# The first block of a fused two-layer product: first strip of w1 in five pieces, x's fourth tile as fp16 on another queue, wide products before narrow ones

## The chip, the core and the metric

The kernel runs on one core of a Trainium2 chip. The metric is the device time of one execution in microseconds (us), as the median of several runs; lower is better. A core has TensorE (PE in the rows; PEld is its weight load), VectorE (DVE), ScalarE (ACT), GpSimd (POOL) and SyncE (SP). SP, ACT and POOL can issue transfers (DMAs), each on a queue of its own, and all queues are served by the same 16 DMA engines.

## The reference

```python
x: (16, 512, 768)   w1: (768, 3072)   b1: (3072,)   w2: (3072, 768)      # all float32
y = np.matmul(x, w1) + b1
y = np.maximum(y, 0)
return np.matmul(y, w2).astype(np.float32)
```

## The kernel before

x is one matrix of 8192 x 768. Its rows are taken in 8 blocks of 1024, and the hidden width of 3072 in two chunks of 1536, so there are 16 iterations. In each of them a first layer (from x and w1 to y, with the bias and the maximum) is followed by a second layer (from y and w2 to the output). From the second iteration on both layers use fast matrix multiplication: DVE builds sums of blocks of x, w1, y and w2, and PE multiplies the sums (lines L1101 for the first layer, L1229 for the second). These sums need all blocks of a matrix, which at the start are not there yet, so the first layer of the first block is computed plainly (`first_block`, matmuls at L998) while the data come in.

What the first block needs, and the names that the rows use:

- The 1024 rows of x are 8 tiles of 128 rows. Tiles 0 to 3 (`rows`, kept in `s`) are loaded as fp32, tiles 0 and 2 by SP's queue, 1 and 3 by ACT's (L722). PE transposes each tile in six 128x128 pieces (L938), three to a bank of PSUM; DVE turns the first bank into fp16 (`x<-ps`, L946), ACT the second (L944). Tiles 4 to 7 (`xn`) come by POOL's queue, which converts fp32 to fp16 on the way, two tiles in a transfer (L717).
- The first chunk of w1 is six strips of 768 x 256 (`v1`), which POOL's queue converts to fp16 as well (L696). A strip is six blocks of 128 rows (k2 = 0 or 1, three k each). Strips 0 and 1 come in two halves, the others whole.
- w2 comes as twelve pieces behind them (L702), then the next block of x (L717).
- A strip gives two column groups of y (j = 0, 1). For each, six weight blocks are multiplied with x's tiles 0 to 3 (m = 0) and later with tiles 4 to 7 (m = 1). `plain(strip, j, m, parts)` records that: with parts = 2 the four tiles are two matmuls of 256 columns for each weight block, with parts = 1 one matmul of 512 columns. ACT then adds the bias and takes the maximum (L1006). For strips 0 and 1 the steps for k2 = 0 are put ahead of those for k2 = 1 (`split`).
- While it waits for the first tile PE multiplies a tile of ones (L739).

The order of the work is not written out by hand alone. `first_block` and the others record tasks in PE's order; a planner (`Graph.run`) places all tasks in time by a cost of each, and times at which data of the start are expected are given to it as `presets`. Each engine then runs its tasks in the planned order and waits on semaphores, so that these times move no transfer; they only set which task stands ahead of which on DVE and ACT. The transfers of the start are issued in `prologue`, in the order in which they are written there. POOL's queue has eight semaphores, and its ninth transfer is issued when the first has landed.

`constants` makes the unit matrices for the transposes, the tile of ones and, with eight fills on POOL (L681, L682), two tables of limits that a check of the input's size uses at the end of the kernel.

Of the kernel before, what the change touches and what calls it, by code (L numbers as in the profile page):

```python
# [131 lines left out]
LAST_POOL = (0, 1, 3)  # L132

EARLY = 5

# [460 lines left out]
class Fast:  # L596
# [66 lines left out]
    def constants(self):  # L663
        nc = self.nc
        nw1, nw2, nx, nb = self.NCH * 12, self.NCH * 16, self.M // P, self.H // P
        self.ident = self.const.tile([P, P], FP32, name="ident")
# [9 lines left out]
        self.high = self.const.tile([P, n], FP32, name="high")  # L676
        self.low = self.const.tile([P, n], FP32, name="low")
        at = 0
        for width, hi, lo in ((nw1, W1_HI ** 4, W1_LO ** 4), (nw2, W2_HI ** 2, W2_LO ** 2),
# [32 lines left out]
    def load_x(self, it, half, parts=1):  # L712
        m0 = self.block(it) * self.MB + half * 512
        r = self.xf[m0:m0 + 512, :].rearrange("(s p) k -> p s k", p=P)
        for n in range(parts):
            a, b = 4 // parts * n, 4 // parts * (n + 1)
            self.nc.gpsimd.dma_start(out=self.xn[:, 4 * half + a:4 * half + b], in_=r[:, a:b])  # L717

    def prologue(self):
# [18 lines left out]
        for _ in range(9):  # L738
            nc.tensor.matmul(self.ps[:, 7, 0:P], lhsT=self.ones, rhs=self.ones, start=True,  # L739
                             stop=True)  # L740

    def presets(self):
        g = self.g
        for t, at in enumerate((9.45, 11.45, 13.45, 15.45, 17.45, 24.0)):
            for k in range(2):
                g.preset(("w1", t // 3, 2 * (t % 3) + k), at - (0 if t > 1 or k else 0.9))
        for q in range(4):
            for h in range(3):
                for n in range(2):
                    g.preset(("w2", 2 * q + n, h), 25.05 + 3 * q + h + (0.3 if 3 * q + h > 5 else 0))  # L750
        for s in range(4):
            g.preset(("xn", 4 + s), 19.35 if s < 2 else 21.95)
            g.preset(("xn", s), 39.5)
            g.preset(("rows", s), (5.3, 5.3, 7.2, 7.2)[s])
        g.preset("b1_rows", 6.0)
# [167 lines left out]
    def add_transpose_first(self, half, s):  # L923

        for a in range(2):
            ps = Reg("ps", leaves=0)

            def view(ps=ps):
                p = self.ps[:, ps.at[0], :]
                if half:  # L930
                    p = p[:, 0:3 * P // 2].bitcast(FP16)
                return p[:, 0:3 * P].rearrange("p (k m) -> p k m", k=3)

            def turn(a=a, view=view):
                ident = (self.ident, self.ident16)[half]
                rows = self.xn[:, 4 + s, :] if half else self.s[:, s]
# [11 lines left out]
            self.g.add("PE", 210 if half else 380, turn, writes=[ps],  # L948
                       reads=[("xn", 4 + s)] if half else [("rows", s), self.hold[s]])
# [3 lines left out]
    def add_bias(self):  # L953
# [7 lines left out]
        def tables(after):  # L961
# [22 lines left out]
        return tables  # L984

    def plain(self, strip, j, m, parts=1, split=False):
# [37 lines left out]
    def first_block(self):  # L1024
        for s in range(4):
            self.add_transpose_first(0, s)
            if s == 1:
                tables = self.add_bias()
# [24 lines left out]
        for p in late[1:]:  # L1053
            next(p)
        run(*late, self.plain(1, 1, 1, 2),
            *(self.plain(strip, j, 1, 2 if strip == 2 else 1)
              for strip in range(2, EARLY) for j in range(2)))
        run(*(self.plain(strip, j, m) for strip in range(EARLY, 6) for m in range(2)
              for j in range(2)))

# [483 lines left out]
    def build(self):  # L1544
        self.place_all()
        self.plan()
        self.g.run(begin=5.0)
        return self
# [60 lines left out]
```

## Time and profile before

| | us |
|---|---|
| median of 3 runs | 846.82 (846.67 to 847.12) |
| the profiled execution | 846.81 |
| its span, from the first to the last instruction | 845.1 |
| PE busy | 838.5 (99%) |
| DVE busy | 735.7 (87%) |
| ACT busy | 567.3 (67%) |
| the first matmul of the second layer starts at | 41.23 |

The profile is that of one execution. Its own time is 1.7 us above its span, and 0.01 us below the median, so that a sum made on the profile can be held against the median as it is. An engine that is 99% busy sets the time where nothing but its own work stands between its instructions; what it waits for has to be read in the stretch where it waits.

### The profile page before, as it was taken

Reading aid. Unit: us, or ns where it says so; the run is one execution under the profiler, and the core shown is the slowest. Engines: PE = TensorE matmul, PEld = TensorE weight load, DVE = VectorE, ACT = ScalarE, POOL = GpSimd, SP = SyncE. Lnnn points to the kernel's source line nnn. Section 1 sums busy time; section 2 is a strip of 40 time slices with the busy share of each in tenths; the row PEclk is TensorE's granted clock in tenths of the full one; section 3 lists DMA queues with packets and bytes.
Section 4 is the critical chain, followed back from the end, with each engine's and each line's share of the span. In section 5 each row is a group of like instructions: output and inputs, shape, how many; then the busy total and the mean of one; then the engine's idle time right before and its main releaser. Section 6 shows DMA issues by size and latency. Waiting matters only on the chain.

```text
span 845.1 us, 16822 instructions
## 1 busy us (share of the span) xinstructions
PE 838.5 (99%) x6383; PEld 625.4 (74%) x6383; DVE 735.7 (87%) x1229; ACT 567.3 (67%) x1199; POOL 172.5 (20%) x186
## 2 busy tenths in 40 slices
PE   9999999999999999999999999999999999999997
PEld 7668778686786867768687686877868678686874
DVE  5899988969789697988999979798896979979787
ACT  4866876779677684856858568766757666456462
POOL 6210011102011010110031503324041240501303
PEclk9999999999999999999999999999999999999999
DMA  9997498978988678593893977979789797986926
GB/s 210 205 180 189 84 221 115 166 180 132 215 113 162 158 133 190 104 226 136 238 176 67 190 127 123 186 106 178 127 128 147 118 172 113 143 138 76 177 86 169
DMA packets 171127, 128.93 MB, mean 153 GB/s; under 512 B 93964, under 2 KB 169508, under 8 KB 171044
## 3 DMA queue, kind: packets, MB, share of 16 engines
q0 software_dynamic: 56592, 68.82, 53.2%
q1 hardware_dynamic: 113984, 58.02, 29.0%
q8 instruction: 50, 0.82, 0.4%
q10 hardware_dynamic: 468, 1.00, 0.3%
q14 instruction: 33, 0.27, 0.1%
HBM read 73.54 MB, written 69.21 MB: 169 GB/s over the span
## 4 chain that ended last, share of the span: by engine, by line
PE 99%; DMA 1%; ACT 0%; issue 0%; ACTq 0%
PE ps L1229 48%; PE ps L1101 47%; PE ps L998 4%; DMA s<-in_x_dram 1%; PE ps L938 1%; ACT s L1240 0%; PE ps L958 0%; PE ps L1427 0%; PE ps L1438 0%; ACTq L1240 0%
## 5 line engine op out<-in xcount | busy, mean ns | idle before, releaser
L1229 PE MATMUL ps<-v,y 128*128 128x384 f16 x2496 | 408.2, 326 | 0.0
L1101 PE MATMUL ps<-x,v 128*128 128x256 f16 x3600 | 395.6, 273 | 0.0
L1101 PEld LDWEIGHTS <-v 128*128 128x128 f16 x3600 | 352.2, 98 | 42.3
L1229 PEld LDWEIGHTS <-y 128*128 128x128 f16 x2496 | 244.2, 98 | 159.9
L1240 ACT ACTIVATE s<-ps 128x384 f32<-128x384 f32 (+1 forms) x245 | 153.1, 643 | 125.4 <-PE ps L1229 124.9
L1073 DVE TENSOR_TENSOR y<-y 128x768 f16<-128x768 f16 (+1 forms) x384 | 219.0, 617 | 2.5
L1144 DVE CUSTOM_DVE_ANT_0 y<-ps,s 128x512 f16<-128x512 f32 x240 | 155.9, 685 | 52.9 <-ACT s L1141 40.1
L1281 POOL DMA_DIRECT2D out_dram<-s x78 | 93.9, 1475 | 144.8 <-ACT s L1240 91.8
L1141 ACT ACTIVATE s<-ps,bt 128x256 f32<-128x256 f32 x180 | 75.1, 469 | 62.8 <-PE ps L1101 56.5
L841 DVE TENSOR_TENSOR x<-x 128x768 f16<-128x768 f16 (+1 forms) x210 | 113.4, 577 | 1.2
L1141 ACT ACTIVATE y<-ps,bt 128x256 f16<-128x256 f32 x180 | 69.4, 485 | 10.8 <-PE ps L1101 10.8
L1240 ACT ACTIVATE ps<-ps 128x384 f32<-128x384 f32 (+1 forms) x143 | 67.0, 507 | 6.5 <-PE ps L1229 3.2
L1246 DVE TENSOR_TENSOR s<-ps,s 128x768 f32<-128x768 f32 x74 | 70.5, 952 | 0.9
L717 POOL DMA_DIRECT2D xn<-in_x_dram x30 | 25.9, 863 | 213.3 <-DMA x<-xn 101.0
L1246 DVE TENSOR_TENSOR s<-s,ps 128x768 f32<-128x768 f32 x60 | 57.0, 950 | 2.1
L780 ACT ACTIVATE junk<-xn 128x768 f16<-128x768 f16 x64 | 53.9, 843 | 0.3
L1284 POOL DMA_DIRECT2D out_dram<-s x15 | 17.8, 1184 | 168.6 <-ACT s L1240 156.9
L1141 ACT ACTIVATE ps<-ps,bt 128x256 f32<-128x256 f32 x60 | 26.7, 445 | 32.4 <-PE ps L1101 31.4
L1137 ACT ACTIVATE ps<-ps 128x512 f32<-128x512 f32 x60 | 35.3, 588 | 4.8 <-DVE y L1144 4.0
L1152 DVE TENSOR_TENSOR s<-s,ps 128x512 f32<-128x512 f32 x30 | 20.6, 687 | 17.8 <-PE ps L1101 17.8
L998 PE MATMUL ps<-x,v 128*128 128x256 f16 (+1 forms) x216 | 31.8, 308 | 0.0
L1147 DVE SCALAR_TENSOR_TENSOR s<-ps,bt,s 128x256 f32<-128x256 f32 x60 | 26.1, 476 | 4.4 <-PE ps L1101 4.4
(61 smaller groups left out, 310.0 us busy)
## 6 DMA issues: line engine op xcount, KB each, us to landing
out_dram<-s POOLq DMA_DIRECT2D x93, 384.0 KB, 8.6
out_dram<-s SPq DMA_DIRECT2D x69, 384.0 KB, 7.0
xn<-in_x_dram POOLq DMA_DIRECT2D x28, 768.0 KB, 9.6
v<-in_w_dram POOLq DMA_DIRECT2D x16, 192.0 KB, 7.6
x<-out_dram SPq DMA_DIRECT2D x14, 192.0 KB, 2.4
w1d<-in_w_dram POOLq DMA_DIRECT2D x6, 384.0 KB, 6.6
w2d<-in_w_dram POOLq DMA_DIRECT2D x12, 192.0 KB, 5.0
v<-w1d SPq DMA_DIRECT2D x12, 192.0 KB, 4.8
```

The source lines that it names most:

```text
L780: self.nc.scalar.activation(out=self.junk, in_=self.xn[:, s, :], func=ACTF.Square, accum_out=self.stat[:, self.stat_at["x"] + i:][:, 0:1])
L841: self.nc.vector.tensor_tensor(out=self.two(x, out), in0=self.two(x, in0), in1=self.two(x, in1), op=ALU.add if sign > 0 else ALU.subtract)
L998: nc.tensor.matmul(self.ps[:, ps.at[0], cols], lhsT=self.v1[:, gi, 2 * h + k2, k, j * P:(j + 1) * P], rhs=rhs, start=(first and k2 == 0 an ...
L1073: self.nc.vector.tensor_tensor(out=self.two(self.y, out), in0=self.two(self.y, in0), in1=self.two(self.y, in1), op=ALU.add if sign > 0 els ...
L1101: nc.tensor.matmul(self.ps[:, at, j * self.QM:(j + 1) * self.QM], lhsT=self.v1[:, gi, self.w1s[c][gi][FIRST_V[p]], k, j * P:(j + 1) * P], ...
L1137: nc.scalar.activation(out=out, in_=ps, scale=float(a), func=func if kind == "out" else ACTF.Copy)
L1141: nc.scalar.activation(out=out[:, j], in_=ps[:, j], func=func, scale=float(a), bias=beta(j))
L1144: nc.vector._custom_dve(TENSOR_ADD_SAT, out=out, in0=ps, in1=s, s0=F_MAX, s1=0.0)
L1229: nc.tensor.matmul(self.ps[:, bank[ch].at[j], 0:NH], lhsT=self.y[:, ys[SECOND_U[p]], m0:m0 + P], rhs=self.v2[:, slot[SECOND_V[p]], h, :], ...
L1240: nc.scalar.activation(out=out, in_=ps, func=ACTF.Copy, scale=float(a))
L1246: engine.tensor_tensor(out=out, in0=in0, in1=in1, op=ALU.add if a == b else ALU.subtract)
L1281: nc.gpsimd.dma_start(out=rows, in_=out, accum_op=ALU.add)
```

## The change

All of it lies in the first block.

- x's tile 0 is loaded in two halves of 384 columns, one by SP's queue and one by ACT's. Tiles 1 and 2 both go by SP's queue. Tile 3 goes by POOL's queue, behind the first piece of w1, and is converted to fp16 on the way; its transposes and copies are then fp16 like those of tiles 4 to 7.
- Strip 0 of w1 comes in five pieces: blocks 0, 1, 2 and 3 of 128 rows one by one, blocks 4 and 5 together. Strips 1 and 2 come in halves, the others whole. All six strips stand ahead of x's tiles 4 to 7 (before, the last strip stood behind them).
- The eight fills of the limit tables move behind all these issues (`limits`).
- The products of strip 0 are a function of their own, `plain_first`. The first block of weights is multiplied with tiles 0 to 2 as soon as it is there (256 and 128 columns), then tile 3 is transposed, and the parts of tile 3 follow by themselves (128 columns); the second half of the strip is done 512 columns at a time.
- Strips 1 and 2 are done 512 columns at a time for tiles 0 to 3. For tiles 4 to 7, nine of the twelve column groups take 256 columns at a time (before, six).
- The matmuls of ones are 4 of 256 columns, where they were 9 of 128.

```diff
     def prologue(self):
         nc = self.nc
-        for s in range(4):
-            (nc.sync, nc.scalar)[s % 2].dma_start(out=self.s[:, s],
-                                                  in_=self.xf[s * P:(s + 1) * P, :])
-            if s == 1:
-                self.load_bias()
+        for q, a in ((nc.sync, 0), (nc.scalar, self.K // 2)):
+            q.dma_start(out=self.s[:, 0, a:a + self.K // 2], in_=self.xf[0:P, a:a + self.K // 2])
+        for s in (1, 2):
+            nc.sync.dma_start(out=self.s[:, s], in_=self.xf[s * P:(s + 1) * P, :])
+        self.load_bias()
         self.constants()
-        self.load_strip(self.v1, 0, 0, 0, 2)
-        self.load_strip(self.v1, 0, 0, 1, 2)
-        for strip in range(2, EARLY):
-            self.load_strip(self.v1, 0, *divmod(strip, 3))
+        v = self.v1[:, 0, 0:2].rearrange("p a k h -> p (a k) h")
+        w1r = self.w1.rearrange("(k p) h -> p k h", p=P)
+        for k, n in ((0, 1), (1, 1), (2, 1), (3, 1), (4, 2)):
+            nc.gpsimd.dma_start(out=v[:, k:k + n], in_=w1r[:, k:k + n, 0:2 * P])
+            if k == 0:
+                nc.gpsimd.dma_start(out=self.row_tile(3), in_=self.xf[3 * P:4 * P, :])
+        for h in (1, 2):
+            self.load_strip(self.v1, 0, 0, h, 2)
+        for h in range(3):
+            self.load_strip(self.v1, 0, 1, h)
         self.load_x(0, 1, 2)
-        for strip in range(EARLY, 6):
-            self.load_strip(self.v1, 0, *divmod(strip, 3))
+        self.limits()
...
+    def plain_first(self):
...
+        for k in range(3):
+            for j in range(2):
+                product(j, 0, k, ((0, 2), (2, 1)))
+            if k == 0:
+                self.add_transpose_first(0, 3)
+        for j in range(2):
+            for k in range(3):
+                product(j, 0, k, ((3, 1),))
+        for j in range(2):
+            product(j, 1, 0, ((0, 4),))
+        for j in range(2):
+            for k in (1, 2):
+                product(j, 1, k, ((0, 4),))
...
-        for strip in range(2):
-            pair = [self.plain(strip, j, 0, 2, True) for j in range(2)]
-            for p in 4 * pair:
+        self.plain_first()
+        for strip in (1, 2):
+            pair = [self.plain(strip, j, 0, 1, True) for j in range(2)]
+            for p in 2 * pair:
                 next(p)
             run(*pair)
-        early = [self.plain(strip, j, 0, 2 if strip == 2 else 1)
-                 for strip in range(2, EARLY) for j in range(2)]
+        early = [self.plain(strip, j, 0) for strip in range(3, 6) for j in range(2)]
```

POOL, at the start of the program, before: the fills of the limit tables (`high`, `low`), then the issues of w1 (`v_65`), of x's tiles 4 to 7 (`xn`) and of the last strip.

```order
L669 CAST ident_88<-ident 128x128
L681 MEMSET high 128x24
...
L682 MEMSET low 128x24
L696 DMA v_65<-in_w_dram 128x3x256 x4
L696 DMA v_65<-in_w_dram 128x6x256 x3
L717 DMA xn<-in_x_dram 128x2x768 x2
L696 DMA v_65<-in_w_dram 128x6x256
L702 DMA v_66<-in_w_dram 128x2x384 x12
```

The same place after the change.

```order
L667 CAST ident_88<-ident 128x128
L736 DMA v_65<-in_w_dram 128x256
L738 DMA s<-in_x_dram 128x768
L736 DMA v_65<-in_w_dram 128x256 x3
L736 DMA v_65<-in_w_dram 128x2x256
L698 DMA v_65<-in_w_dram 128x3x256 x4
L698 DMA v_65<-in_w_dram 128x6x256 x3
L719 DMA xn<-in_x_dram 128x2x768 x2
L683 MEMSET high 128x24
```

The first issue of w1 now follows the unit matrices directly; one issue of x (`s`, tile 3) has come in behind it, and the last strip has moved ahead of `xn`.

PE, at the start of the program, before: the ones, the transposes of tiles 0 and 1, the bias, the transposes of tiles 2 and 3, then the first products.

```order
L739 MATMUL ps<-ones 128x128 x9
L938 MATMUL ps<-ident,s 128x128 x12
L958 MATMUL ps<-ident,b_rows 128x24
L938 MATMUL ps<-ident,s 128x128 x12
L998 LDWEIGHTS v_65
L998 MATMUL ps<-x,v_65 128x256
```

The same place after the change.

```order
L751 MATMUL ps<-ones 128x256 x4
L953 MATMUL ps<-ident,s 128x128 x12
L973 MATMUL ps<-ident,b_rows 128x24
L953 MATMUL ps<-ident,s 128x128 x6
L1008 LDWEIGHTS v_65
L1008 MATMUL ps<-x,v_65 128x256
L1008 LDWEIGHTS v_65
L1008 MATMUL ps<-x,v_65 128x128
...
L953 LDWEIGHTS s
L953 MATMUL ps<-ident_88,s 128x128
```

Six transposes of fp32 have gone from ahead of the first product; the fourth tile's transposes now stand behind the first block's products, as fp16, and PE waits there for that tile.

DVE, from the end of the bias tables on, before: sums of w1 (`v_65`), copies of x's tiles 4 to 7 (`x<-ps`), sums of w2 (`v_66`) and of y.

```order
L857 TENSOR_TENSOR v_65<-v_65 128x768 x12
L946 COPY x<-ps 128x3x128 x4
L857 TENSOR_TENSOR v_65<-v_65 128x768 x10
L875 TENSOR_TENSOR v_66<-v_66 128x1152
L1073 TENSOR_TENSOR y<-y 128x768
```

The same place after the change.

```order
L871 TENSOR_TENSOR v_65<-v_65 128x768 x18
L961 COPY x<-ps 128x3x128 x2
L1126 TENSOR_TENSOR y<-y 128x768
L871 TENSOR_TENSOR v_65<-v_65 128x768 x3
L961 COPY x<-ps 128x3x128 x2
L1126 TENSOR_TENSOR y<-y 128x768 x3
L871 TENSOR_TENSOR v_65<-v_65 128x768
```

Six more sums of w1 stand ahead of the first copies of tiles 4 to 7, and sums of y have moved up among them. From a little way into the second iteration on, the order of all engines is what it was.

## Rows read from the trace of the kernel before

**Rows 1.** The page, busy time of each engine, share of the span, instructions.

```profile
PE 838.5 (99%) x6383; PEld 625.4 (74%) x6383; DVE 735.7 (87%) x1229; ACT 567.3 (67%) x1199; POOL 172.5 (20%) x186
```

**Rows 2.** Chain that ended last, in order of time: start us, us, what.

```profile
0.98 4.54 DMA s<-in_x_dram
5.52 0.14 issue
...
41.39 25.35 PE ps L1229 x156
```

**Rows 3.** PE's waits from 5 us to the end: us in total, times, longest.

```profile
PE ps L938 <- DMA s<-in_x_dram: 0.7, 1, 0.7
```

**Rows 4.** Timeline of PE, 4 to 42 us: start, us, line, xcount.

```profile
8.62 11.91 PE L998 MATMUL ps<-x,v 128*128 128x256 f16 x90
20.37 0.83 PE L938 MATMUL ps<-ident,xn 128*128 128x128 f16 x12
21.04 2.11 PE L998 MATMUL ps<-x,v 128*128 128x512 f16 x12
...
41.23 0.98 PE L1229 MATMUL ps<-v,y 128*128 128x384 f16 x5
```

**Rows 5.** Stretches of DMA, 2 to 7 us: DMA share and GB/s stand last.

```profile
2.00:3.70 1.70, 1.70 (x9) 1.00 0.83 231
3.70:4.70 1.00, 1.00 (x2) 1.00 1.03 403
4.70:5.70 1.00, 1.00 (x3) 1.00 1.00 393
```

**Rows 6.** DMA queues, 2 to 6 us (first two) and 6 to 7 us.

```profile
q1 hardware_dynamic: 286, 0.78, 58.3%
q10 hardware_dynamic: 214, 0.51, 35.2%
...
q0 software_dynamic: 101, 0.05, 37.6%
```

**Rows 7.** DMA issues one by one (windows): KB, us from issue to landing.

```profile
v<-in_w_dram POOLq DMA_DIRECT2D x1, 192.0 KB, 6.2
v<-in_w_dram POOLq DMA_DIRECT2D x1, 192.0 KB, 6.4
w2d<-in_w_dram POOLq DMA_DIRECT2D x1, 192.0 KB, 3.6
v<-in_w_dram POOLq DMA_DIRECT2D x1, 384.0 KB, 9.1
v<-in_w_dram POOLq DMA_DIRECT2D x1, 384.0 KB, 11.1
```

**Rows 8.** Timeline of POOL, 0.9 to 9 us.

```profile
1.85 0.11 POOL L681 MEMSET high<- 128x24 f32 x1
...
2.35 5.78 POOL L696 DMA_DIRECT2D v<-in_w_dram  x7
```

**Rows 9.** Timeline of DVE from 4 us.

```profile
6.22 1.21 DVE L946 CAST x<-ps 128x384 f16<-128x384 f32 x2 [4.98 <-PE ps L938]
...
24.16 5.27 DVE L857 TENSOR_TENSOR v<-v 128x768 f16<-128x768 f16 x10
```

**Rows 10.** DMA queues, 15 to 16 us.

```profile
q8 instruction: 1, 0.02, 6.1%
```

**Rows 11.** Stretches of DVE: us, busy (xcount).

```profile
20.00:24.00 4.00, 1.35 (x5) 1.00 1.35 199
...
30.20:68.00 37.80, 37.45 (x59) 1.00 1.10 196
```

**Rows 12.** Stretches of PE's matmuls of ones: us, busy (xcount), PEclk.

```profile
1.29:4.25 2.96, 2.96 (x14) 1.00 0.67 209
4.25:5.00 0.75, 0.72 (x6) 1.00 1.02 395
```

More of the change, by code (lines that the diff above doesn't have):

```diff
@@ L132 @@
 LAST_POOL = (0, 1, 3)
-EARLY = 5
 X_FUSE = (3,)
@@ L664, in constants @@
         nc = self.nc
-        nw1, nw2, nx, nb = self.NCH * 12, self.NCH * 16, self.M // P, self.H // P
+        nb = self.H // P
         self.ident = self.const.tile([P, P], FP32, name="ident")
@@ L677, in constants, with limits @@
         self.low = self.const.tile([P, n], FP32, name="low")
+    def limits(self):
+        nc = self.nc
+        nw1, nw2, nx, nb = self.NCH * 12, self.NCH * 16, self.M // P, self.H // P
         at = 0
@@ L737, in prologue @@
         self.load_x(1, 0)
-        for _ in range(9):
-            nc.tensor.matmul(self.ps[:, 7, 0:P], lhsT=self.ones, rhs=self.ones, start=True,
-                             stop=True)
+        ones = self.ones.rearrange("p (a m) -> p a m", a=1).to_broadcast([P, 2, P])
+        for _ in range(4):
+            nc.tensor.matmul(self.ps[:, 7, 0:2 * P].rearrange("p (a m) -> p a m", a=2),
+                             lhsT=self.ones, rhs=ones, start=True, stop=True)
     def presets(self):
         g = self.g
-        for t, at in enumerate((9.45, 11.45, 13.45, 15.45, 17.45, 24.0)):
+        for t, at in enumerate((9.85, 11.85, 13.9, 15.9, 17.95, 20.0)):
             for k in range(2):
-                g.preset(("w1", t // 3, 2 * (t % 3) + k), at - (0 if t > 1 or k else 0.9))
+                g.preset(("w1", t // 3, 2 * (t % 3) + k), at - (0 if t > 2 or k else 1.0))
+        for k, at in enumerate((7.2, 8.2, 8.55, 8.95, 9.85, 9.85)):
+            g.preset(("w1k", k), at)
         for q in range(4):
@@ L749, in presets @@
                 for n in range(2):
-                    g.preset(("w2", 2 * q + n, h), 25.05 + 3 * q + h + (0.3 if 3 * q + h > 5 else 0))
+                    g.preset(("w2", 2 * q + n, h), 25.4 + 0.98 * (3 * q + h))
         for s in range(4):
-            g.preset(("xn", 4 + s), 19.35 if s < 2 else 21.95)
+            g.preset(("xn", 4 + s), 22.1 if s < 2 else 24.3)
             g.preset(("xn", s), 39.5)
-            g.preset(("rows", s), (5.3, 5.3, 7.2, 7.2)[s])
+            g.preset(("rows", s), (4.5, 5.5, 6.6, 7.85)[s])
         g.preset("b1_rows", 6.0)
@@ L923, in add_transpose_first @@
     def add_transpose_first(self, half, s):
+        short = half or s == 3
         for a in range(2):
@@ L929, in view @@
                 p = self.ps[:, ps.at[0], :]
-                if half:
+                if short:
                     p = p[:, 0:3 * P // 2].bitcast(FP16)
@@ L934, in turn @@
             def turn(a=a, view=view):
-                ident = (self.ident, self.ident16)[half]
-                rows = self.xn[:, 4 + s, :] if half else self.s[:, s]
+                ident = self.ident16 if short else self.ident
+                rows = self.xn[:, 4 + s, :] if half else self.row_tile(s)
                 for k in range(3):
@@ L947, in add_transpose_first @@
             r = 2 * half + s // 2
-            self.g.add("PE", 210 if half else 380, turn, writes=[ps],
+            self.g.add("PE", 210 if short else 380, turn, writes=[ps],
                        reads=[("xn", 4 + s)] if half else [("rows", s), self.hold[s]])
@@ L984, in add_bias, with product, fn, evict @@
         return tables
+    def plain_first(self):
+        nc = self.nc
+        banks = [Reg("ps", leaves=2) for _ in range(2)]
+        def product(j, k2, k, tiles):
+            def fn():
+                for s, width in tiles:
+                    nc.tensor.matmul(
+                        self.ps[:, banks[j].at[0], s * P:(s + width) * P],
+                        lhsT=self.v1[:, 0, k2, k, j * P:(j + 1) * P],
+                        rhs=(self.x[:, k2:k2 + 3:2, k, :] if width == 4 else
+                             self.x[:, s // 2 * 2 + k2, k, s % 2 * P:(s % 2 + width) * P]),
+                        start=(k2 == 0 and k == 0 and s == 0),
+                        stop=(k2 == 1 and k == 2), skip_group_check=True)
+            n = sum(width for _, width in tiles)
+            self.g.add("PE", 54 * n, fn,
+                       reads=[("w1k", 3 * k2 + k)]
+                       + [("x", t // 2 * 2 + k2, t % 2) for s, width in tiles
+                          for t in range(s, s + width)], writes=[banks[j]])
+        def evict(j):
+            nc.scalar.activation(
+                out=self.y[:, j:j + 5:4, 0:self.QM],
+                in_=self.ps[:, banks[j].at[0], :].rearrange("p (a m) -> p a m", a=2),
+                func=ACTF.Relu, bias=self.b1y[:, j:j + 1])
+        for k in range(3):
[11 more added lines that the diff above has]
+                product(j, 1, k, ((0, 4),))
+            self.g.add("ACT", 692, lambda j=j: evict(j), reads=[banks[j], "b1y"],
+                       writes=[("y", r * 4 + j, 0) for r in range(2)])
     def plain(self, strip, j, m, parts=1, split=False):
@@ L1024, in first_block @@
     def first_block(self):
-        for s in range(4):
+        for s in range(3):
             self.add_transpose_first(0, s)
@@ L1054, in first_block @@
             next(p)
[L1055 to L1059, printed above, removed]
+        run(*late, *(self.plain(strip, j, 1, 2) for strip, j in ((1, 1), (2, 0), (2, 1), (3, 0), (3, 1), (4, 0))),
+            *(self.plain(strip, j, 1) for strip, j in ((4, 1), (5, 0), (5, 1))))
     def y_keys(self, slot):
@@ L1546, in build @@
         self.plan()
-        self.g.run(begin=5.0)
+        self.g.run(begin=4.0)
         return self
```

2 lines of the change are left out of this document (added).

## The prediction, made before the changed kernel had run

> **What bounds the kernel now.** I read the page's busy times first: PE is busy for 99% of the span, DVE for 87% [rows 1]. That alone does not say that PE sets the time, so the chain of work that ended last comes next. It starts with a transfer of x that is under way from 0.98 to 5.52 us and runs through PE from then on; the second layer starts in it as one unbroken piece [rows 2]. The list of PE's waits closes the case: from 5 us to the end PE's matmuls waited once, 0.7 us, for that transfer [rows 3]. So the kernel is a start of some 8.6 us and then PE's work without a gap. Nothing later can give time back unless PE gets less work; a change of the start is worth what it moves PE's first product, less what it adds to PE's work and to its waits before the second layer. The first product starts at 8.62, the second layer at 41.23 [rows 4]: 32.61 us of gapless work lie between, and only its two ends can be traded.
>
> **When the data come.** In the stretches of DMA the first 1.7 us move 231 GB/s, 393 KB, one tile of x; then 403 and 393 KB for each us [rows 5]. Two tiles are through at 4.7, and the first of them landed at 5.52 [rows 2], 0.8 later. In the changed kernel three tiles go in order instead of four side by side: through at 3.7, 4.7 and 5.7, landed near 4.55, 5.55 and 6.55 by the same 0.8. The halving of tile 0 neither adds nor saves bytes.
>
> POOL's queue is the second supply. Its first issue starts at 2.35 and seven take 5.78, so 0.83 each [rows 8]; the first half strip lands 6.2 after its issue [rows 7], at 8.55. The third issue (at 4.0, 6.4) lands at 10.4, so a half takes 0.95 to 1.0. The sixth (6.5, 9.1) lands at 15.6, two and a half strips later, 2.05 a strip: cutting a strip in two costs nothing that shows. I count 2.0 a strip, 0.33 for a sixth, and 1.0 for a tile of x in fp16, which has half a strip's bytes. With these, the queue behaves before as if it began at 8.55 - 1.0 = 7.55.
>
> How much earlier it begins after the change is the largest unknown. It has to make up 1.0 us, tile 3's share. Bounds: nothing, 7.55, if the begin does not depend on what moves; 3.1 us earlier at most, if the first issue, 0.5 earlier without the fills (1.85 in place of 2.35, [rows 8]), took only the 3.6 that as many bytes (of w2, to memory) take later on a free queue [rows 7]. The queue counts tell which end is nearer: from 2 to 6 us only the two queues of x move packets, and POOL's queue has 101 in the seventh us [rows 6]. The queue waits for x, mostly. x is 393 KB less on those two queues, 1.0 us at 393 KB for each us [rows 5]; the issue is 0.5 earlier. I take the middle, 0.75: the queue begins at 6.8.
>
> The Trainium skill says otherwise of such queues: by its page DMA: Bandwidth & Descriptors, section Queues, rings and completion order, each DMA engine takes its queues in turn, a packet at a time. Here it did not before 6 us, although POOL's first issue had ended by 3.2; the trace decides, and the rule stays as a rival below.
>
> **The sum.** (1) Before the first product PE now transposes tiles 0 to 2. Tile 2 lands at 6.55; 0.14 from landing to PE [rows 2], 0.56 more until DVE's first copy starts (5.66 to 6.22), 0.605 for the copy [rows 9]: 7.85. The first piece of w1, at 6.8 + 0.33 = 7.15, is early; it is tile 2 that the first product waits for. First product: 7.85 in place of 8.62, -0.77.
>
> (2) Tile 3's six transposes now lie behind it: 12 took 20.37 to 21.04 [rows 4], 56 ns each, +0.34.
>
> (3) Wide and narrow matmuls: the 90 of the first stretch are 72 of 256 columns and 18 of 512, so 108 units of 256, and took 11.75 us [rows 4], 109 ns a unit. By the code the columns stay the same and the count falls from 216 to 210; 0.
>
> (4) New gaps, piece by piece. First products of two column groups, 2 x (109 + 56) ns, to 8.18. Tile 3 lands at 7.15 + 1.0 = 8.15: in time, by nothing; to 8.52. Blocks 1 and 2 at 8.5 and 8.8: to 8.85 and 9.18. Tile 3's narrow parts, to 9.5. Block 3 at 9.15, to 9.95; the last two at 9.8, to 10.8. Strip 1's first half lands at 6.8 + 2.0 + 1.0 + 1.0 = 10.8. So the chain is met with no slack at tile 3 and at strip 1, and from there PE takes 2.6 us for a strip where the queue takes 2.0: 0.15 of slack at strip 3, 0.7 at strip 4, 1.25 at strip 5. I put 0.05 for the gaps, +0.05.
>
> (5) DVE must follow. It is busy 37.45 of 37.80 us from 30.2 to 68 [rows 11], so PE 0.4 earlier asks DVE for 0.4. It has that: 2.65 us idle from 20 to 24 [rows 11], because the last strip stands behind x's tiles and its ten sums run from 24.16 on at 0.53 each [rows 9]. All strips now stand ahead of those tiles and land by 20; six more sums fit there. 0, and the loss of the whole gain if not.
>
> Sum: -0.77 + 0.34 + 0.05 = -0.38. On the profiled execution, 846.81 (0.01 below the median), that is **846.4 us**. The same sum with the queue at its bounds: at 7.55, 0.75 later, +0.37; at 1.0 earlier or more the gaps vanish and tile 2 alone decides, -0.43; a tile 2 that lands 0.4 sooner along with it, -0.8.
>
> **The rivals.** *The queue does not begin sooner.* Tile 3's 1.0 us then stands in front of strip 1 and PE waits 0.75 there: 847.2. It decides from 0.4 us of the 0.75. Of the same kind is a strip that is late by itself: the seventh issue (7.3, 11.1) lands at 18.4, 2.8 after the sixth, and in that time one instruction packet of 0.02 MB went through the engines [rows 10]. 0.8 at strip 4 or 5 costs 0.1 at most; at strip 1 or 3 it costs 0.65 to 0.8, 847.2 again. Against it: nothing but the smaller x.
>
> *DVE gives it back.* The idle is filled less than I think, and PE waits at the end of the second layer: 846.8.
>
> *The queues share after all.* ACT's queue is nearly empty after its half tile, so POOL's pieces may enter early; a piece of w1 and tile 3, 1.33 us of the queue, would then pass ahead of tile 2, and the first product comes that much later: 847.8. That is what the page's turns would do. Rows 6 speak against it.
>
> *A piece costs as much as a half strip.* The rows hold no smaller transfer than the half. If a sixth of a strip took its 1.0 as well, strip 0 would take 5.0 instead of 2.0, and PE would wait for it: +3.0, 849.4. It decides from 0.1 a piece. Against it: halves and wholes run at one rate. The Trainium skill speaks for it: in the section Rules for kernel authors of the same page transfers under 64 KB are mostly overhead, and these pieces are 64 KB each. No run here shows one.
>
> *The clock.* 14 matmuls of ones begin in 2.96 us, 0.21 each; the other four fit into the half microsecond behind 4.25 [rows 12]. The clock column has no record that early, but the pace doubles: TensorE climbed from 1.2 to 2.4 GHz there. After the change PE has holes of 0.2 to 0.5 between the tiles. If it fell back and took as long to climb, 2.96 us of half speed cost 1.5: 847.9.
>
> **How the numbers follow.** A measurement of this kernel can tell about 0.2%, 1.7 us, from no change: 845.1 to 848.5. Forecast, 845.9 to 846.8: 0.64. No earlier begin or a late strip, 846.8 to 847.5: 0.17. DVE: 0.07. Sharing: 0.05. Costly pieces: 0.03. Clock: 0.02. Under 845.9: 0.02. The 8 in 10 are reached by 845.9 to 847.2. Slower by over 0.2% are the costly pieces and the worst of the clock, 0.04; faster by it would need PE without any hole from the first tile on and that tile before 4.3, 0.02; the rest, 0.94, is the same.
>
> **What would show it.** Right: in PE's timeline first product near 7.85, started by DVE's copy of tile 2 and not by w1; a short wait of PE for tile 3 or strip 1 or none; the second layer at 40.85; POOL's first landing near 7.15; PE without waits for DVE around 68. Wrong: `s` landing after 7 us for tile 2, pieces of w1 more than 0.4 apart, a wait of PE for `v` near 10.8 above 0.3, or for DVE in the second layer.

## The result, and the profile after

| | before | after |
|---|---|---|
| median of 12 runs each, us | 846.97 (846.41 to 847.59) | 848.72 (847.86 to 850.43) |
| ratio, 95% interval | | 1.0023 [1.0015, 1.0032] |
| the profiled execution | 846.81 | 849.49 |
| its span | 845.1 | 847.6 |
| second layer starts | 41.23 | 41.68 |
| PE's last matmul ends | 840.47 | 841.63 |
| from there to the end of the span | 4.65 | 5.98 |

The change makes the kernel 0.23% slower; forecast was 846.4, in a range of 845.9 to 847.2. The profiled execution is 2.5 us longer in its span, and three places make that up: 0.45 at the start of the second layer, 0.7 near 147 us, and 1.3 behind PE's last matmul, where the forecast had looked for nothing. Outside the span, too, the changed kernel spends some 0.2 us more: its twelve executions take 1.85 us on average beyond their spans, and the kernels below with changed transfers at the start 1.75 to 1.84, those with before's transfers 1.63 to 1.65. No row places that.

The page's busy times of the changed kernel, beside [rows 1]:

```profile
PE 839.7 (99%) x6367; PEld 624.4 (74%) x6367; DVE 736.6 (87%) x1229; ACT 568.0 (67%) x1199; POOL 174.8 (21%) x191
```

PE has 16 matmul records fewer (an fp32 matmul counts as two). Its timeline from the first tile to the second layer (start, us, line, what, count, idle time before it), beside [rows 4]:

```profile
4.87 2.70 PE L953 MATMUL ps<-ident,s 128*128 128x128 f32 x12
...
7.67 0.88 PE L953 MATMUL ps<-ident,s 128*128 128x128 f32 x6
8.38 0.27 PE L1008 MATMUL ps<-x,v 128*128 128x256 f16 x1
8.87 0.38 PE L1008 MATMUL ps<-x,v 128*128 128x128 f16 x3 [0.21 <-DVE x L961]
9.09 0.50 PE L953 MATMUL ps<-ident,s 128*128 128x128 f16 x6
9.42 2.45 PE L1008 MATMUL ps<-x,v 128*128 128x256 f16 x20
11.71 11.82 PE L1054 MATMUL ps<-x,v 128*128 128x512 f16 x54
...
41.68 2.60 PE L1282 MATMUL ps<-v,y 128*128 128x384 f16 x15
```

The first product comes 0.24 earlier than before, the first with tile 2 in it at 8.87; the tile's landing at 7.18 and its transposes hold it, and then DVE's copy. From there PE's list of waits has none up to 41.68. The twelve transposes of tiles 0 and 1 take 2.70 us, where 12 took 1.50 before: in this execution the granted clock is recorded as full only from 7.37 us on.

The list of PE's waits, from 5 us to the end (us in total, times, longest), beside [rows 3]:

```profile
PE ps L1282 <- DVE y L1126: 0.4, 1, 0.4
PE ps L1008 <- DVE x L961: 0.2, 1, 0.2
```

The first of them is the place near 147 us: ahead of it PE's instructions start 0.39 later than before, behind it 1.14. The chain of work leads from there over DVE's sums to a transfer of x under way for 5.22 us from 138.80. No later profile has this wait. Two packets of the queues that carry programs lie in its way: one of PE's (q8, read below) of 1.39 us at 136.91, while the transfer of x ahead of it was under way, and one of another such queue (q14) of 1.40 us at 141.97; the late transfer's last packet moves at 143.41, right behind that one's end. In a_again, the same kernel, the like packets lie at 137.11 and 140.31 and take 0.96 and 0.55 us, and PE does not wait there. So program loading may be behind this place as well; no run tests it.

DMA in stretches (share and GB/s last), then the packets of the two queues from 5 to 6 us, beside [rows 5, 6]:

```profile
3.70:4.70 1.00, 1.00 (x4) 0.79 (x3) 0.00 (x0) 0.00 (x0) 1.00 (x4) 1.00 1.05 417
4.70:5.70 1.00, 1.00 (x5) 0.83 (x4) 0.00 (x0) 0.00 (x0) 1.00 (x3) 1.00 1.03 352
5.70:6.70 1.00, 1.00 (x7) 1.00 (x6) 0.56 (x1) 0.31 (x1) 1.00 (x2) 1.00 1.33 188
6.70:7.70 1.00, 1.00 (x7) 0.70 (x5) 0.56 (x1) 0.27 (x2) 0.31 (x2) 1.00 1.11 162
...
q0 software_dynamic: 130, 0.07, 61.0%
q1 hardware_dynamic: 89, 0.23, 58.3%
```

POOL's queue (q0) starts in the sixth microsecond, while SP's queue (q1) still carries tile 2, and the two share the engines. Before, they were shared in the same way: beside the 101 packets of POOL's queue from 6 to 7 us [rows 6], ACT's queue still moved 103 of tile 3.

```profile
q10 hardware_dynamic: 103, 0.28, 72.7%
```

In the changed kernel 162 to 188 KB move in a microsecond from then on, with the engines no less busy: fp16 on the way out, counted at half its fp32 bytes.

The other end of the program: transfers issued from 836 us to the end, and the queue that carries PE's program (q8) in the one microsecond in which its last packet starts; first before, where these rows were not read,

```profile
out_dram<-s SPq DMA_DIRECT2D x4, 384.0 KB, 3.1
out_dram<-s SPq DMA_DIRECT2D x3, 192.0 KB, 2.6
out_dram<-s ACTq DMA_DIRECT2D x1, 192.0 KB, 2.8
...
q1 hardware_dynamic: 14, 0.02, 6.3%
q8 instruction: 1, 0.02, 5.9%
```

then the changed kernel.

```profile
out_dram<-s SPq DMA_DIRECT2D x4, 384.0 KB, 4.7
out_dram<-s SPq DMA_DIRECT2D x3, 192.0 KB, 4.0
out_dram<-s ACTq DMA_DIRECT2D x1, 192.0 KB, 4.0
...
q1 hardware_dynamic: 199, 0.31, 86.2%
q8 instruction: 1, 0.02, 9.8%
```

The last stores take 1.2 to 1.6 us longer. Before, the last block of PE's program was fetched in 836 to 837 us, a lull of the store queue (14 packets); now in 838 to 839, in the midst of the stores (199 packets). The page counts these packets over the whole execution, 50 in both kernels:

```profile
q8 instruction: 50, 0.82, 0.4%
```

0.82 MB by 50 is 16.4 KB, and 2 x 6367 matmuls and weight loads by 50 is 255 instructions. The Trainium skill, Advanced Engine Details and Errata, section ISA Cache, has cache lines of 16 KB that hold 256 instructions; the trace agrees, with 16.4 KB and 255.

**Theory A**: PE's program is fetched block by block, so a program that is some 35 instructions shorter (16 matmuls, 16 weight loads, 3 waits) reaches each fetch that much later in the work; the last fetch slips among the last stores, and they end the program. **Theory B**: only the first block's transfers cost time, the rest is chance.

### The profile page after: what moved, and what is told of

The parts are those of the page before. It is cut to its first block, busy times and chain, and to the rows that moved or that the text cites. A ratio compares the mean times of both kernels' runs of the same rounds, so it can differ in the third digit from the quotient of the medians.

```text
span 847.6 us, 16791 instructions
## 1 busy us (share of the span) xinstructions
PE 839.7 (99%) x6367; PEld 624.4 (74%) x6367; DVE 736.6 (87%) x1229; ACT 568.0 (67%) x1199; POOL 174.8 (21%) x191
## 4 chain that ended last, share of the span: by engine, by line
PE 98%; DMA 1%; DVE 0%; ACT 0%; issue 0%; SPq 0%; DVEq 0%; ACTq 0%
PE ps L1282 48%; PE ps L1154 46%; PE ps L1054 3%; DMA x<-xn 1%; PE ps L953 1%; PE ps L751 0%; PE ps L1008 0%; DVE y L1197 0%; DVE y L1126 0%; DVE x L855 0%; ACT s L1293 0%; DVE x L961 0%; SPq L786 0%; DVE ones L673 0%; PE ps L973 0%
## 5 line engine op out<-in xcount | busy, mean ns | idle before, releaser
L1054 PE MATMUL ps<-x,v 128*128 128x256 f16 (+1 forms) x186 | 29.1, 317 | 0.0
```

The source lines that it names most:

```text
L1054: nc.tensor.matmul(self.ps[:, ps.at[0], cols], lhsT=self.v1[:, gi, 2 * h + k2, k, j * P:(j + 1) * P], rhs=rhs, start=(first and k2 == 0 an ...
```

## The experiments

Each line is one kernel. "Fetch" is the start of the last packet of PE's program, "ahead by" how far it lies before the end of PE's last matmul, "tail" the time from that end to the end of the span, all from its profile; the medians are of 8 to 12 runs, with the ratio to runs of before on the same chip.

| kernel | PE's matmuls | second layer | PE ends | fetch | ahead by | tail | median | ratio |
|---|---|---|---|---|---|---|---|---|
| before | 6383 | 41.23 | 840.47 | 836.31 | 4.16 | 4.65 | 846.97 | |
| b_again | 6383 | 41.19 | 840.48 | 836.26 | 4.22 | 4.65 | 846.99 | 1.0004 [0.9995, 1.0014] |
| after | 6367 | 41.68 | 841.63 | 838.46 | 3.17 | 5.98 | 848.72 | 1.0023 [1.0015, 1.0032] |
| a_again | 6367 | 41.37 | 840.58 | 837.23 | 3.35 | 6.16 | 848.65 | 1.0022 [1.0013, 1.0031] |
| b_less | 6367 | 41.72 | 840.92 | 837.64 | 3.28 | 5.88 | 848.49 | 1.0023 [1.0014, 1.0032] |
| b_wide3 | 6365 | 41.41 | 840.61 | 837.84 | 2.77 | 5.78 | 848.20 | 1.0016 [1.0007, 1.0025] |
| a_pad | 6383 | 43.43 | 842.63 | 838.04 | 4.59 | 4.64 | 849.06 | 1.0025 [1.0014, 1.0035] |
| a_pos | 6385 | 41.83 | 841.03 | 836.74 | 4.29 | 4.56 | 847.21 | 1.0003 [0.9994, 1.0012] |
| a_early | 6417 | 42.14 | 841.36 | 830.51 | 10.85 | 4.50 | 847.29 | 1.0006 [0.9997, 1.0015] |
| a_wide6 | 6331 | 41.34 | 840.70 | 843.74 | -3.04 | 6.37 | 849.03 | 1.0024 [1.0015, 1.0033] |
| a_nox3 | 6331 | 41.59 | 841.27 | 843.42 | -2.15 | 6.29 | 849.14 | 1.0025 [1.0015, 1.0034] |
| a_order | 6385 | 42.05 | 841.35 | 837.13 | 4.22 | 4.65 | 847.59 | 1.0007 [0.9998, 1.0017] |
| a_halves | 6385 | 41.76 | 840.95 | 836.64 | 4.31 | 4.64 | 847.21 | 1.0004 [0.9994, 1.0013] |
| a_x012 | 6385 | 42.70 | 841.89 | 837.71 | 4.18 | 4.72 | 847.53 | 1.0010 [1.0000, 1.0020] |

Over all fourteen profiles: a fetch 4.1 us or more ahead of PE's end goes with a tail of 4.50 to 4.72, one at 2.7 to 3.4 with 5.78 to 6.16, one behind the end with 6.29 and 6.37. The fetch keeps to a count of PE's instructions, as theory A has it: when the last one starts, PE has started 12,717 to 12,743 of them (matmuls, weight loads and waits) in twelve profiles, and 12,687 of 12,690 in a_wide6 and a_nox3, whose programs are the shortest.

Single executions scatter more than the medians tell. The changed kernel's twelve run from 847.86 to 850.43 and b_less's eleven from 847.21 to 850.55, four of them above 849.7; those of before in the first table end at 847.59, but one of b_again took 849.34. None above 849.5 has a profile, so what the longest ones wait for is not shown.

**a_again and b_again**, the two kernels once more.

> The changed kernel once more, to see which of the late pieces of its profile return. In that profile the second layer began 0.45 us late, PE lost 0.72 more near 144 us behind a transposing load of x, and from the end of ACT's last instruction to the end of the span 5.4 us passed where the kernel before took 4.0. Theory A, instruction loading: PE's program comes in blocks of 16 KB on the same DMA engines, a block lies at a fixed count of PE's instructions, and the changed kernel has fewer of them ahead of every place, so the last block is loaded among the last stores. Then the last load of a block again falls near 838 us, within 4 us of PE's end, the tail is again above 5 us, and the median is near 848.7. Theory B, the first block alone is late and the rest of the profile is chance: the second layer is late again by 0.3 to 0.6, the tail is near 4.0, and a median near 848.7 would not be explained.

> The kernel before once more, for a second profile of it. Theory A: the last block of PE's program is loaded near 836.3 again and the tail is 3.8 to 4.3 us. If the tail were above 5 us here as well, chance would be the better reading. TensorE's clock at the start: in the first profile it was at its upper level from 4.26 us on, in the changed kernel from 7.37; if it rises later here, the moment is not a matter of the change.

Both repeat their medians. The changed kernel's second profile has the tail again, but neither the late clock nor the wait near 147 us. With before's start, too, the moment at which the clock is recorded as full varies: 4.26 us in the first profile, 4.94 in b_again and 6.17 in b_wide3 below.

**a_pad**, the changed kernel with the length of PE's program put back by other matmuls of ones.

```diff
-        ones = self.ones.rearrange("p (a m) -> p a m", a=1).to_broadcast([P, 2, P])
-        for _ in range(4):
-            nc.tensor.matmul(self.ps[:, 7, 0:2 * P].rearrange("p (a m) -> p a m", a=2),
-                             lhsT=self.ones, rhs=ones, start=True, stop=True)
+        for _ in range(12):
+            nc.tensor.matmul(self.ps[:, 7, 0:85], lhsT=self.ones, rhs=self.ones[:, 0:85],
+                             start=True, stop=True)
```

> The changed kernel with twelve matmuls of ones of 85 columns in place of four of 256: the same columns, but as many PE instructions ahead of every product as the kernel before, to within three. Theory A: the last block of PE's program is loaded near 836.5 again, before the last stores; the tail goes back to about 4.0 us, the wait near 144 us is gone or smaller, and the median falls by 1.0 to 1.8, to 847.0 to 847.7. What is left is the first block, 0.3 to 0.5 above the kernel before. Theory B: no change, 848.2 to 849.0.

By the time A failed here; the profile shows why. The last fetch lies 4.59 us ahead of PE's end, and the tail is back at 4.64, but twelve fp32 matmuls of ones took 5.41 us instead of 3.78, the transposes waited for them until 6.50, and the second layer starts 2.2 late. The padding cost what it gave back.

**b_less**, the kernel before with a shorter program.

```diff
-        for _ in range(9):
-            nc.tensor.matmul(self.ps[:, 7, 0:P], lhsT=self.ones, rhs=self.ones, start=True,
-                             stop=True)
+        ones = self.ones.rearrange("p (a m) -> p a m", a=1).to_broadcast([P, 2, P])
+        for _ in range(4):
+            nc.tensor.matmul(self.ps[:, 7, 0:2 * P].rearrange("p (a m) -> p a m", a=2),
+                             lhsT=self.ones, rhs=ones, start=True, stop=True)
...
-        early = [self.plain(strip, j, 0, 2 if strip == 2 else 1)
+        early = [self.plain(strip, j, 0, 2 if strip == 2 and j == 0 else 1)
```

> The kernel before with 32 PE instructions fewer and nothing else of the change: four matmuls of ones of 256 columns, and one column group of strip 2 as one matmul of 512 columns for each weight block. All loads stay as they were. Theory A: the last block of PE's program is loaded near 838, the tail grows from 4.0 to above 5 us, and the median rises by 0.8 to 1.8, to 847.8 to 848.8. Theory B: as the kernel before, within 0.4 us of 847.0.

As A said: with none of the change's transfers it is as slow as the changed kernel. In its profile 1.23 us of that lie in the tail and 0.49 ahead of the second layer, where x's fourth tile landed at 8.30 instead of 7.79. But its matmuls of ones are the changed kernel's, so the shape of these could still be the cause.

**b_wide3** shortens the program of before without touching its start.

```diff
-        run(*late, self.plain(1, 1, 1, 2),
-            *(self.plain(strip, j, 1, 2 if strip == 2 else 1)
-              for strip in range(2, EARLY) for j in range(2)))
+        run(*late, self.plain(1, 1, 1),
+            *(self.plain(strip, j, 1) for strip in range(2, EARLY) for j in range(2)))
```

> The kernel before, with one edit that leaves its first 24 us alone: the last three half products of the second half that still went as two of 256 columns (strip 1's second row block, both of strip 2) go as one of 512. The columns are the same, the matmuls 18 fewer, PE's program 36 instructions shorter, as in the changed kernel. Theory A (a block of PE's program is fetched every 256 instructions; 36 fewer push the last fetch among the last stores): second layer starts at 41.2 as before, last fetch at 837.2 to 838.5 instead of 836.3, the stores issued from 836 on take 4 to 4.8 us instead of 2.5 to 3.4, time from PE's last instruction to the end 5.9 to 6.2 instead of 4.65, the whole 848.1 to 848.6. Theory B (the loss lies in the first block's transfers and the rest is chance): 846.9, end 4.65 after PE's last.

PE ends within 0.14 of before, and the tail is 1.1 longer. The first fetch, ahead of the edit, starts where before's does (15.39 us, before 15.49); the third, behind it, is late (54.52, before 51.50). Same views as above, stores from 836 us and the microsecond of the last fetch:

```profile
out_dram<-s SPq DMA_DIRECT2D x4, 384.0 KB, 4.5
out_dram<-s SPq DMA_DIRECT2D x3, 192.0 KB, 3.8
out_dram<-s ACTq DMA_DIRECT2D x1, 192.0 KB, 4.0
...
q1 hardware_dynamic: 201, 0.31, 87.5%
q8 instruction: 1, 0.02, 5.9%
```

The packet itself takes as long as before (5.9% of 16 engines in one us, 0.94 us of one engine). What differs in these rows is the traffic that it falls into, 201 packets of the stores against 14. The ones and the first block's transfers are out as causes of this part. How a packet of 0.95 us makes the stores 1.2 us and more late is not shown.

**a_pos**, the changed kernel with its program lengthened by matmuls that fit into PE's idle start.

```diff
-        ones = self.ones.rearrange("p (a m) -> p a m", a=1).to_broadcast([P, 2, P])
-        for _ in range(4):
-            nc.tensor.matmul(self.ps[:, 7, 0:2 * P].rearrange("p (a m) -> p a m", a=2),
-                             lhsT=self.ones, rhs=ones, start=True, stop=True)
+        for _ in range(8):
+            nc.tensor.matmul(self.ps[:, 7, 0:P], lhsT=self.ones, rhs=self.ones, start=True,
+                             stop=True)
+        short = self.ones.bitcast(FP16)
+        for _ in range(10):
+            nc.tensor.matmul(self.ps[:, 7, 0:32], lhsT=short[:, 0:P], rhs=short[:, 0:32],
+                             start=True, stop=True)
```

> The changed kernel with 8 warm-up matmuls of 128 columns and 10 of 32 columns in fp16 instead of 4 of 256: PE's program is 36 instructions longer, one more than what the change took off, and the warm-up ends at about the same time (4.9 to 5.1). Theory A: last fetch back at 836 to 837, end 4.65 after PE's last, the whole 847.0 to 847.4. Theory B: 848.6. If the warm-up's shape itself matters (the clock's rise), the first product moves and with it the second layer's start by up to 1 us either way.

The loss is gone: 847.21, a ratio of 1.0003. Its last stores and last fetch:

```profile
out_dram<-s SPq DMA_DIRECT2D x4, 384.0 KB, 3.0
out_dram<-s SPq DMA_DIRECT2D x3, 192.0 KB, 2.5
out_dram<-s ACTq DMA_DIRECT2D x1, 192.0 KB, 2.9
...
q1 hardware_dynamic: 89, 0.11, 33.1%
q8 instruction: 1, 0.02, 5.9%
```

**a_early** shifts the fetch further ahead. Its edit stands here against a_pos.

```diff
-        for _ in range(8):
+        for _ in range(4):
...
-        for _ in range(10):
+        for _ in range(50):
```

> The changed kernel with 4 warm-up matmuls of 128 columns and 50 of 32 columns in fp16: PE's program is 100 instructions longer than the changed kernel's, 64 longer than with the padding that put its length back. Theory A: the last program block is fetched some 3 us earlier still, 833 to 835, before the stores of the last 5 us are issued; they take 2.3 to 3.0 us, the end comes 4.5 to 4.65 after PE's last instruction, the whole 846.9 to 847.3. A fetch that comes earlier than before's buys nothing more, since the last two stores bound the end. Theory B: 848.6.

The tail is 4.50, the stores take 2.4 to 2.9: a fetch that is out of their way altogether buys 0.15 over before in this one profile. It came at 830.51, earlier than the 833 to 835 that I wrote. The first fetch of this kernel, at 12.21 us, fell on a half of strip 2, which landed 1.1 later than in a_again (14.50, 13.41), and PE waited 0.4 for it.

**a_wide6** goes the other way, in order to have no last fetch.

```diff
-        run(*late, *(self.plain(strip, j, 1, 2) for strip, j in ((1, 1), (2, 0), (2, 1), (3, 0), (3, 1), (4, 0))),
+        run(*late, *(self.plain(strip, j, 1) for strip, j in ((1, 1), (2, 0), (2, 1), (3, 0), (3, 1), (4, 0))),
```

> The changed kernel with its six remaining pairs of 256 columns outside xn's first three (strips 1 to 4 of the second half) as single matmuls of 512: 36 matmuls and 72 instructions of PE fewer still. Theory A: the program is then too short for the fiftieth fetch (it starts no earlier than at instruction 12,705 and the program ends at 12,690), so the last stores are undisturbed: 4.65 or less from PE's last instruction to the end, the whole 847.0 to 847.4, within 0.1 per cent of before. Theory B: no effect on the end, 848.6.

A miss: there is a fiftieth fetch all the same, at 843.74, behind PE's last matmul. Its stores from 836 us and that microsecond (q10 is ACT's store queue):

```profile
out_dram<-s SPq DMA_DIRECT2D x4, 384.0 KB, 2.7
out_dram<-s SPq DMA_DIRECT2D x3, 192.0 KB, 2.5
out_dram<-s ACTq DMA_DIRECT2D x1, 192.0 KB, 4.7
...
q10 hardware_dynamic: 132, 0.18, 50.3%
q1 hardware_dynamic: 48, 0.05, 15.7%
q14 instruction: 2, 0.02, 7.1%
q8 instruction: 1, 0.02, 6.3%
```

All stores issued well ahead of it are as quick as in a_early; the very last one, on ACT's queue, takes 4.7 instead of 2.9, and it ends the program. The two packets of q14 come at the like place in before (843.64 and 843.71), whose last stores are not late. That refutes "no fetch" and supports A the more: the delay sits where the fetch sits.

**a_nox3** asks what holds the first block. On a_wide6, x's fourth tile is not loaded (its transposes read the third, in fp32), so part of the output is another.

```diff
-        return self.s[:, s, 0:self.K // 2].bitcast(FP16) if s == 3 else self.s[:, s]
+        return self.s[:, min(s, 2)]
...
-            if k == 0:
-                nc.gpsimd.dma_start(out=self.row_tile(3), in_=self.xf[3 * P:4 * P, :])
...
```

> The same as the kernel with the six wide pairs, but x's fourth tile is not loaded; its transposes read the third tile instead (fp32, 0.3 us longer), so part of the result is another. What it asks: is the first block held by the fourth tile's landing at 8.64? If so, the pieces of w1 land 1.2 us sooner, PE's waits of 0.4 to 1.0 us after its first product go down to the 0.2 of VectorE's copies, and the second layer starts 0.3 to 0.8 us earlier than in the kernel with the tile: 846.4 to 846.9. If VectorE's copies or the strips' landings hold the block instead, the start stays within 0.2 us.

The pieces of w1 came 0.9 sooner (the second at 7.74 instead of 8.63), but the second layer starts at 41.59, against 41.34; 0.3 of that is the longer transposes. So nothing is gained without tile 3 in these two executions: tile 2 landed in them at 7.31 and 7.38, and it holds the first product.

The last three stand on a_pos. **a_order** puts tile 2's first parts behind tile 3's transposes.

```diff
-                product(j, 0, k, ((0, 2), (2, 1)))
+                product(j, 0, k, ((0, 2), (2, 1)) if k else ((0, 2),))
             if k == 0:
                 self.add_transpose_first(0, 3)
+                for j in range(2):
+                    product(j, 0, 0, ((2, 1),))
```

> The changed kernel with its program's length put back, and the two first products on x's third tile moved behind the fourth tile's transposes, so that PE does not wait for VectorE's copy of the third tile right after its first product. If that copy is what cost 0.2 to 0.4 us, the second layer starts 0.2 to 0.3 us sooner for the same landings (first product to second layer 33.0 instead of 33.2 to 33.7 us). If the fourth tile's landing is behind it, PE waits the same at the transposes and nothing is gained. The whole 846.9 to 847.3, not to be told from 847.2 by the times.

PE then waits the same 0.2 at the transposes for the same copies, and from the first product to the second layer it takes 33.6 us, not 33.0. The expected gain did not come.

**a_halves** loads the first strip in two halves again.

```diff
-        for k, n in ((0, 1), (1, 1), (2, 1), (3, 1), (4, 2)):
+        for k, n in ((0, 3), (3, 3)):
```

> The changed kernel with its program's length put back, and the first strip of w1 in two halves again (as before, three k-blocks each) with the fourth tile behind the first half. If a piece costs what its bytes cost, the first half lands 0.7 us later than the first piece did (at 7.6 to 8.1), the fourth tile at 8.9 to 9.1, the second half at 10.0, and the second layer starts 0 to 0.4 us later (41.4 to 42.0). If the five pieces cost overhead, the last of the strip lands sooner than 10.1 to 10.4 by 0.3 or more and the second layer starts sooner.

The first half lands at 8.13, tile 3 at 9.05, the second half at 10.03. With five pieces the strip is complete at 10.07 in a_pos, and at 10.07 to 10.42 over the seven profiles with x's transfers as changed; so the five pieces cost at most 0.4 us, and one profile of the halves tells no more. In the time they neither cost nor gain what shows: the medians are 847.21 both.

**a_x012** loads x's first three tiles as before the change.

```diff
-        for q, a in ((nc.sync, 0), (nc.scalar, self.K // 2)):
-            q.dma_start(out=self.s[:, 0, a:a + self.K // 2], in_=self.xf[0:P, a:a + self.K // 2])
-        for s in (1, 2):
-            nc.sync.dma_start(out=self.s[:, s], in_=self.xf[s * P:(s + 1) * P, :])
+        for s in range(3):
+            (nc.sync, nc.scalar)[s % 2].dma_start(out=self.s[:, s],
+                                                  in_=self.xf[s * P:(s + 1) * P, :])
```

> The changed kernel with its program's length put back, and x's first three tiles as before the change: whole, in turn on SP's, ACT's and SP's queue. If three transfers in a row on SP's queue make the third tile late (6.5 to 7.4), it lands at 6.6 or sooner now, with the first two at 5.1 to 5.6, and the first product comes at 7.4 to 7.7. If the third tile is late because POOL's queue starts before it is done, it lands at 6.6 to 7.4 all the same. Second layer 41.2 to 41.7 either way, the whole 846.8 to 847.4.

Tile 2 lands at 6.56, but tiles 0 and 1 only at 5.5 and 5.7; the first product comes at 8.20, and the second layer at 42.70, later than I allowed, after short waits for x, for w1 (twice) and for copies (twice). Neither of these two orders of x's tiles reaches the forecast.

## Why the prediction was wrong

**The step that failed** is term (3), "By the code the columns stay the same and the count falls from 216 to 210; 0", and with it the sentence that nothing later can give time back unless PE gets less work. The columns do stay the same. But the six products and the shorter row of ones take 16 matmul records and as many weight loads off PE's program (35 instructions with the waits), and that moves the last fetch from 836.3 to between 837.2 and 838.5. Measured cost: a tail of 5.98 and 6.16 instead of 4.65, so +1.3 to +1.5 us, most of the 1.75 between the medians. b_wide3 shows it without the change, a_pos and a_early the change without it, a_wide6 at a third place. [Rows 10] had such a packet in view, as the reason for a late strip; I did not ask where its 50 fellows would fall. The prediction's sum ended at the second layer and carried the rest over; how long the stores take behind PE's last matmul was never read.

**The first block** was mis-sized, by some 0.5 to 0.8: +0.45 and +0.15 in the two profiles (a_wide6 +0.11) where the sum had -0.38. Executions with before's transfers scatter too (41.19 to 41.72 in four), so the sign of so little is not certain; the time of a_pos, +0.3 us by its ratio with an interval from -0.5 to +1.0, says the same. By its terms:

- (1) Tile 2 at 6.55 and its first product at 7.85: 7.18 and 8.87 in the profiled run, 6.65 and 7.89 in a_again. The chain from landing to product was right where PE was free (1.24 in a_again, 1.30 forecast; 1.69 in the profiled run, behind the slow transposes); the landing was not steady. With the first strip in five pieces and the tiles as changed it ranges from 6.36 to 7.73 over seven profiles. POOL's queue was to have its first piece landed at 7.15; that came at 7.37 and, in a_again, at 6.94, and the queue's first packet moved 0.65 earlier than before (5.45, before 6.10; 0.75 was taken), so this size was near. Its reason was not: "The queue waits for x, mostly" is not borne out. The first packet moves 3.60 us after the first issue here and 3.75 before, 3.4 to 4.1 in all fourteen profiles, and x's packets run on beside it. That is the rival *the queues share*, and what the prediction read as its absence before 6 us was a queue that had not begun. The Trainium skill's page DMA: Bandwidth & Descriptors, section Queues, rings and completion order, has each DMA engine take its queues in turn, a packet at a time; the trace agrees as far as that packets of both queues move in the same microsecond (130 and 89), and no row shows the turns themselves. A tile 2 at 7.18 is 0.6 later than forecast. Sharing alone does not make that: a_again has 127 and 91 packets in that microsecond and its tile 2 at 6.65. What delays the last packets is not shown.
- (2) Six transposes, +0.34: 9.09 to 9.42, right.
- (4) Gaps, +0.05: none in the profiled run; 0.4 for tile 3 in a_again, where tile 2 was early. Tile 3 lands at 8.64 in both and was put at 8.15, 1.0 behind the first piece. It came 1.27 behind it in the profiled run and 1.70 in a_again: at the 162 to 188 KB a microsecond of these stretches, 197 KB of fp16 take 1.05 to 1.2, and over the seven profiles that load it this way it lands from 8.28 to 8.64, whether the first piece came at 6.59 or at 7.91. So in these profiles an early tile 2 can run into tile 3, and a late one covers it; an earlier tile 2 alone gains little.
- (5) DVE follows, 0: right but for the 0.4 near 147 us in the profiled run and 0.2 for another step of DVE in a_nox3; the other profiles of this block have no wait for DVE's sums.

**The other rivals.** *A piece costs as much as a half strip*: false; pieces land 0.35 to 0.40 apart in the profiled run (8.96, 9.31, 9.71), where a half takes 1.0, and a_halves has its strip at most 0.4 sooner. *The clock*: it was recorded as full at 7.37 instead of 4.26 in the profile (7.18 in a_halves, 9.39 in a_pad), but in a_again at 4.16, which is as slow, so it does not carry the result. *A late strip by itself*: it exists, and goes with a program fetch. a_pos has the first fetch at 15.95 and strip 4 at 19.25; a_again has the fetch at 20.12 and that strip at 18.37. In twelve of the fourteen profiles the transfer of POOL's queue that is under way at the first fetch lands 0.4 to 1.2 us later than the spacing of its neighbours; in a_again and a_pad (fetch at 17.17) none does, and why is not shown. In a_pos it cost 0.3 to 0.4 at the second layer.

**The chances.** Slower by over 0.2% had 0.04, and its cases were costly pieces and the clock; the mechanism that did it was in none. No kernel here beats before by what can be told.

## What to carry to other kernels

When a change alters the number of instructions on an engine with a long unrolled program, look in the trace at where the fetches of its program fall, before and after, above all among the last stores: here 32 to 36 instructions fewer, with the same columns, cost 1.1 to 1.5 us, and padding that fits into PE's idle start gave it back. An edit at the start should be judged with that position put back, otherwise the end answers for it. And read a kernel's tail as a stage of its own, with the latency of each of its last stores.

## What the runs showed of the hardware

- The last 16.4 KB packet of PE's program took 0.95 to 1.8 us. Where it fell among the last stores (six profiles), the store in flight took 1.3 to 1.9 us longer than its like in before, and in the four where others were issued behind it these stayed late to the end of the program.
- The last of the 50 fetches came even when PE had no matmul left (843.74, 3.0 us after the last one's end).
- The recorded rise to the full clock came at 7.37 us in one execution of the changed kernel and at 4.16 in another, and their second layers started 0.3 apart.
- The first packet of POOL's queue, which converts fp32 to fp16, moved 3.4 to 4.1 us after the first issue started, in all fourteen profiles.
- Ten fp16 matmuls of 32 columns took 0.47 us, 50 took 1.54; twelve fp32 matmuls of 85 columns took 5.41: padding was cheap in fp16, not in fp32.
